# mLSTM gate maxima through DRAM and a broadcast DMA per head instead of TensorE products

## The chip, the cores and the metric

The kernel runs on one core of one Trainium2 chip. The metric is the device time of one execution in microseconds; for the kernel before it is the median of three runs. A core has five engines with a queue of instructions each: TensorE (PE, whose weight loads are shown as PEld), VectorE (DVE), ScalarE (ACT), GpSimd (POOL) and SyncE (SP). An engine takes its queue in order: an instruction that waits holds everything behind it. DMAs are issued from SP's queue (weights) and from POOL's (side loads, adding loads, reloads).

## The reference

One layer of a hybrid decoder on x of 512 tokens by 1024 columns, in fp32: a half-step SwiGLU, a mixer that runs dilated attention and an mLSTM side by side, and a second half-step SwiGLU. The change lies in the mLSTM, four heads of 256 columns:

```python
def step(carry, inp):                      # one chunk, all heads
    b = jnp.cumsum(ft, axis=-1)            # ft = log_sigmoid(forget gate), it = input gate
    D = jnp.where(causal, b[..., :, None] - b[..., None, :] + it[..., None, :], -jnp.inf)
    m_inter = b + m[..., None]
    m_t = jnp.maximum(m_inter, jnp.max(D, axis=-1))
    w = jnp.exp(D - m_t[..., None]) * jnp.einsum('bhtk,bhsk->bhts', qt, kt)
    inter = jnp.exp(m_inter - m_t)
    num = jnp.einsum('bhts,bhsv->bhtv', w, vt) + inter[..., None] * jnp.einsum('bhvk,bhtk->bhtv', C, qt)
    den = jnp.sum(w, axis=-1) + inter * jnp.einsum('bhk,bhtk->bht', n, qt)
    h = num / jnp.maximum(jnp.abs(den), jnp.exp(-m_t))[..., None]
```

The kernel treats the 512 tokens as one chunk. With F the running sum of the log forget gates and c = i - F, the weight of source s for target t is exp(c_s - G_t), where G_t is the running maximum of c (from 0); so all the weights of a head need G of every target on all 128 partitions that hold sources.

## The kernel before

The program is one long stream of TensorE work. Products are made in split precision: a matrix x is held as a rounded high part (xh, from a ScalarE cast) and a low part (xl, from a VectorE subtraction), and a product is xh·wh + xl·wh + xh·wl. Weights arrive by SP in slots wf (three), are cast into wh and wl (five of each), and are used 24 products at a time with 512 columns each. Two steps of a Strassen-like scheme save products in places, among them the value/gate projection of the mLSTM (`wide_seven`, tiles vo0p and vo1p, L940), which handles two heads at a time and adds blocks by accumulating DMAs on POOL's queue (vo_x0h, vo_x0l, vo_x; L894, L921).

What stands around the change, in order of the program:

- `gates()` (L1261) transposes the gate columns onto four partitions (one per head), computes F (Fc) and c (cc), and scans the running maxima Gm (L1275). Its tiles ga, gb4 and gc4 hold four partitions; gc4, which contains Gm, is the first tile of the tag gain, which has two buffers in the work pool. The second is selr: a selector matrix, loaded from in_sel, and beside it Gh, the rounded high part of Gm (L1276). Gl is the low part (L1277). The third tile of the tag is hg, the mLSTM gain (L1304), and the fourth and fifth are part5h and part5l (L1568), token parts that are reloaded from DRAM for the branch gates.
- `m_decay(h)` (L1404) spreads the head's row of maxima over 128 partitions with two products: selr has four rows, so selr's columns of head h times Gh, plus the same times Gl, gives G in all partitions of a PSUM bank pb. VectorE adds the causal mask (caus) into gd (L1409), one 128 x 128 square per diagonal block; ScalarE takes seven exponentials into E, four from gd (L1413) and three from pb (L1416), of 384, 256 and 128 columns, with c as bias.
- `m_scores(h)` (L1420) computes query-key products into three banks (pa), VectorE multiplies them into E, ScalarE casts Eh (L1435), VectorE subtracts El (L1436).
- `m_out(h)` (L1439) multiplies by the values (po), and VectorE, ScalarE and a small power on POOL (r_m, L1463) normalise; the squares go to a junk tile jm, which shares the one buffer of the tag gd. The result replaces so, and `m_turn(h)` transposes it on PE into pml (L1481).
- `m_qk_proj` and `m_qk_conv` (L1098, L1107) project (pm) and convolve the next head's queries and keys: z on ScalarE, three multiply-adds on VectorE, tanh, then the casts.

E has one buffer, in turn with the tile vo_E of the projection, so head 0's and head 2's exponentials can begin only when vo_E has been read. PSUM has eight banks in one ring of tiles: a new tile waits for the tile that was taken eight before it.

The kernel is written head by head (L1515 to L1573), but every engine's own order is set when the program is built: a scheduler lines up what is ready, subject to a few explicit orders (`issue_after`). Moving one operation can therefore move others.

Of the kernel before, what the change touches and what calls it, by code (L numbers as in the profile page):

```python
# [10 lines left out]
F32 = mybir.dt.float32  # L11
F32R = mybir.dt.float32r
BF16 = mybir.dt.bfloat16
AF = mybir.ActivationFunctionType
ALU = mybir.AluOpType

P = 128
T = 512
NT = T // P
D = 1024  # L20
# [8 lines left out]
MH = 4  # L29
# [10 lines left out]
def tile_hybrid_block(ctx: ExitStack, tc: tile.TileContext, a: dict):  # L40
    nc = tc.nc
# [16 lines left out]
    work = Work()  # L58
# [3 lines left out]
    def bank(name):  # L62
        return psum.tile([P, 512], F32, tag="pp", name=name)

    def pair(name):
        return [bank(f"{name}_{b}") for b in range(2)]
# [67 lines left out]
    dram = ctx.enter_context(tc.tile_pool(name="dram", bufs=1, space=bass.MemoryType.DRAM))  # L134
# [658 lines left out]
    mix = mctx.enter_context(tc.tile_pool(name="mix", bufs=1, side="right"))  # L793
# [15 lines left out]
    masks = ap_.tile([P, 512], BF16, name="masks")  # L809
    with tc.issue_after(mixer_from):  # L810
        nc.gpsimd.dma_start(masks, a["masks"])
    perm = ap_.tile([P, 2 * P + 8], F32, name="perm")
# [185 lines left out]
    def scores(h):  # L998
        q = [qk_of[h, g] for g in range(3)]
        ps0, ps1 = pair(f"ps0{h}"), pair(f"ps1{h}")  # L1000
        for tb in range(NT):
            lo = 0 if tb else P
            nc.tensor.matmul(ps0[tb // 2][:, tb % 2 * 256 + lo:(tb % 2 + 1) * 256], lhsT=q[0][:, 0, tb * P:(tb + 1) * P],
                             rhs=q[0][:, 1, max(tb - 1, 0) * P:(tb + 1) * P], start=True, stop=True)
        for g in (1, 2):
            for j in range(NT):
                o = j % 2 * 256 + (g - 1) * P
                nc.tensor.matmul(ps1[j // 2][:, o:o + P], lhsT=q[g][:, 0, j * P:(j + 1) * P], rhs=q[g][:, 1, j * P:(j + 1) * P], start=True, stop=True)
        sm = ap_.tile([P, 8, 256], F32, tag="sm", bufs=1, name=f"sm{h}")
        val = small.tile([P, 2, 8], F32, tag="val", name=f"val{h}")  # L1010
        nm = small.tile([P, 8], F32, tag="nm", name=f"nm{h}")
        for half, ps in enumerate((ps0, ps1)):
            for i in range(NT):
                lo = P if half == 0 and i == 0 else 0
                nc.vector.tensor_tensor_reduce(out=sm[:, 4 * half + i, lo:], in0=ps[i // 2][:, i % 2 * 256 + lo:(i % 2 + 1) * 256],
                                               in1=masks[:, half * 256 + lo:(half + 1) * 256], scale=1.0, scalar=NEG,
                                               op0=ALU.add, op1=ALU.max,
                                               accum_out=val[:, 0, 4 * half + i:4 * half + i + 1])
            hs = slice(4 * half, 4 * half + 4)
            nc.vector.tensor_scalar(nm[:, hs], val[:, 0, hs], -SC, None, op0=ALU.mult)  # L1020
        for i in range(8):
            lo = P if i == 0 else 0
            nc.scalar.activation(sm[:, i, lo:], sm[:, i, lo:], AF.Exp, scale=SC, bias=nm[:, i:i + 1],
                                 accum_out=val[:, 1, i:i + 1])
        return sm, val
# [227 lines left out]
    gi, lf = ga[:, 0, :], ga[:, 1, :]  # L1253
    Fc, cc = gb4[:, 0, :], gb4[:, 1, :]
    ones4, Gm = gc4[:, 0, :], gc4[:, 1, :]
    selr = work.tile([4, D], F32R, tag="gain", bufs=2, name="selr")
    Gh = selr[:, 512:1024]
    Gl = mix.tile([4, T], F32R, name="Gl")
    cT = mix.tile([P, 32], F32, name="cT")

    def gates():  # L1261
        pg = pair("pgate")
        for j in range(NT):
            for b in range(2):
                nc.tensor.transpose(pg[b][0:4, j * P:(j + 1) * P], gts[:, j, 4 * b:4 * b + 4], ident)
        nc.scalar.activation(gi, pg[0][0:4, :], AF.Identity, bias=gb[:, 0:1])
        nc.scalar.activation(Gm, pg[1][0:4, :], AF.Identity, bias=gb[:, 1:2])
        nc.vector.scalar_tensor_tensor(lf, Gm, -1.0, Gm, op0=ALU.mult, op1=ALU.max)
        nc.scalar.activation(lf, lf, AF.Exp, scale=-1.0)
        nc.scalar.activation(lf, lf, AF.Ln, bias=1.0)  # L1270
        nc.vector.scalar_tensor_tensor(lf, Gm, 0.0, lf, op0=ALU.min, op1=ALU.subtract)
        nc.vector.memset(ones4, 1.0)
        nc.vector.tensor_tensor_scan(Fc, ones4, lf, 0.0, op0=ALU.mult, op1=ALU.add)
        nc.vector.tensor_tensor(cc, gi, Fc, op=ALU.subtract)
        nc.vector.tensor_tensor_scan(Gm, cc, cc, 0.0, op0=ALU.max, op1=ALU.max)  # L1275
        nc.vector.tensor_copy(Gh, Gm)  # L1276
        nc.vector.tensor_tensor(Gl, Gm, Gh.bitcast(F32), op=ALU.subtract)  # L1277
        nc.vector.tensor_tensor(Fc, Fc, Gm, op=ALU.add)
        nc.scalar.activation(Fc, Fc, AF.Exp, scale=-1.0)

    def gates_turn():
        ptg = bank("ptg")
# [2 lines left out]
            nc.tensor.transpose(ptg[:, 16 + sb * 4:20 + sb * 4], Fc[:, sb * P:(sb + 1) * P], ident[0:4, 0:4])  # L1285
        nc.vector.tensor_copy(cT, ptg[:, 0:32])

    nc.gpsimd.dma_start(selr[:, 0:512], a["sel"])
    caus = mix.tile([P, 1, P], F32, name="caus")
    with tc.issue_after(mixer_from):  # L1290
        nc.gpsimd.dma_start(caus[:, 0, :], a["caus"])
    for h in range(1, HEADS):
        qk_proj(h, 0)
        exchange(h - 1, sm, val)
        qk_proj(h, 1)
        pT = turn(h - 1, sm)
        if h == 3:
            gates_turn()
        qk_proj(h, 2)
        values(h - 1, pT, v12s[(h - 1) // 2])  # L1300
        if h == 2:
            gates()
            hg = work.tile([P, 1, D], F32, tag="gain", bufs=2, name="hg")
            nc.gpsimd.dma_start(hg[:, 0, :], a["mlstm_head_g"].partition_broadcast(P))  # L1304
        sm, val = scores(h)
    pqs = [m_qk_proj(0, 0, lambda: exchange(3, sm, val))]
    tail = []
# [89 lines left out]
    def raw_o(h):  # L1397
        sos[h] = new_so(h)
        for j in range(NT):
            take_o(h, sos[h], j, raw[h][j // 2][:, j % 2, :])  # L1400

    OFF = (0, 512, 1024, 896)

    def m_decay(h):  # L1404
        gbc = bank(f"pb{h}")
        nc.tensor.matmul(gbc, lhsT=selr[:, h * P:(h + 1) * P], rhs=Gh, start=True, stop=False)
        nc.tensor.matmul(gbc, lhsT=selr[:, h * P:(h + 1) * P], rhs=Gl, start=False, stop=True)
        gd = mm.tile([P, NT, P], F32, tag="gd", bufs=1, name=f"gd{h}")
        nc.vector.tensor_tensor(gd, gbc.rearrange("p (a b) -> p a b", b=P), caus.broadcast_to([P, NT, P]), op=ALU.add)  # L1409
        E = mm.tile([P, 1280], F32, tag="E", bufs=1, name=f"E{h}")  # L1410
        for sb in range(NT):
            bias = cT[:, sb * 4 + h:sb * 4 + h + 1]
            nc.scalar.activation(E[:, OFF[sb]:OFF[sb] + P], gd[:, sb, :], AF.Exp, scale=-1.0, bias=bias)  # L1413
            n = T - (sb + 1) * P
            if n:
                nc.scalar.activation(E[:, OFF[sb] + P:OFF[sb] + P + n], gbc[:, (sb + 1) * P:], AF.Exp,  # L1416
                                     scale=-1.0, bias=bias)
        return E

    def m_scores(h, qk, E):  # L1420
        pa = [bank(f"pa{h}{i}") for i in range(3)]
        for sb in range(NT):
            n = T - sb * P
            out = pa[OFF[sb] // 512][:, OFF[sb] % 512:OFF[sb] % 512 + n]
            terms = [(x, y, dk) for x, y in ((0, 0), (0, 1), (1, 0)) for dk in range(2)]
# [255 lines left out]
def _consts():  # L1681
    half = 16
    inv = np.power(np.float32(500000.0), -(np.arange(half, dtype=np.float32) * np.float32(2.0) / np.float32(32.0)))
    ang = np.arange(T, dtype=np.float32)[None, :] * inv.astype(np.float32)[:, None]
    c, s = np.cos(ang).astype(np.float32), np.sin(ang).astype(np.float32)
    import ml_dtypes

    def rope(u, v):
        r = np.concatenate([u, v])
        return np.concatenate([r, r.reshape(32, P, 4).transpose(0, 2, 1).reshape(32, T)])[:, None, :]  # L1690

    p = np.arange(P)[:, None]
    i = np.arange(P)[None, :]
    masks = np.zeros((P, 512), np.float32)
    masks[:, 0:128] = np.where(p - (i - P) <= 128, 0.0, NEG)
    masks[:, 128:256] = np.where(p - i >= 0, 0.0, NEG)
    masks[:, 256:384] = masks[:, 128:256]
    masks[:, 384:512] = np.where((p - i >= 0) & ((p - i) % 4 == 0), 0.0, NEG)
    perm = np.zeros((P, 2 * P + 8), np.float32)
    c4 = np.arange(4)[None, :]  # L1700
    perm[:, 0:P] = p % 32 == i // 4
    perm[:, P:2 * P] = p // 4 == i % 32
    perm[:, 2 * P:2 * P + 4] = p % 4 == c4
    perm[:, 2 * P + 4:] = p // 32 == c4
    sel = np.zeros((4, MH * P), np.float32)
    for h in range(MH):
        sel[h, h * P:(h + 1) * P] = 1.0
    caus = np.where(np.arange(P)[None, :] >= p, 0.0, -NEG).astype(np.float32)
    return {
        "ropeC": rope(c, c), "ropeS": rope(-s, s),  # L1710
        "masks": masks.astype(ml_dtypes.bfloat16), "sel": sel, "caus": caus, "perm": perm,
    }


# [70 lines left out]
```

## Time and profile before

| | |
|---|---|
| median of the runs | 1314.66 us (1314.62 to 1315.81, 3 runs) |
| the profiled execution's own time | 1315.28 us |
| its span, first to last instruction | 1313.3 us |
| PE busy | 1305.4 us |
| VectorE busy | 1041.0 us |
| ScalarE busy | 657.9 us |
| GpSimd busy | 116.3 us |
| granted TensorE clock | 0.999 |
| data moved by DMA | 181.59 MB |

The span is what the trace shows; some 2 us of the execution lie around it. Rows of the timeline give the start in us, the duration, the engine, the line, the operation, the tiles (out<-in), the shape and how many were merged; in brackets stands how long the engine was idle before and what released it. Matmuls overlap, so the time that a matmul takes from the stream is the distance from its start to the next one's, not its duration. Lists of one tile give minimum, median and maximum of the durations in ns. Lists of DMA issues give the size and the median time from issue to landing.

### The profile page before, as it was taken

Reading aid. Unit: us, or ns where it says so; the run is one execution under the profiler, and the core shown is the slowest. Engines: PE = TensorE matmul, PEld = TensorE weight load, DVE = VectorE, ACT = ScalarE, POOL = GpSimd, SP = SyncE. Lnnn points to the kernel's source line nnn. Section 1 sums busy time; section 2 is a strip of 40 time slices with the busy share of each in tenths; the row PEclk is TensorE's granted clock in tenths of the full one; section 3 lists DMA queues with packets and bytes.
Section 4 is the critical chain, followed back from the end, with each engine's and each line's share of the span. In section 5 each row is a group of like instructions: output and inputs, shape, how many; then the busy total and the mean of one; then the engine's idle time right before and its main releaser. Section 6 shows DMA issues by size and latency. Waiting matters only on the chain.

```text
span 1313.3 us, 20816 instructions
## 1 busy us (share of the span) xinstructions
PE 1305.4 (99%) x8189; PEld 1180.7 (90%) x8189; DVE 1041.0 (79%) x1601; ACT 657.9 (50%) x1065; POOL 116.3 (9%) x168
## 2 busy tenths in 40 slices
PE   9999999999999999999999999999999999999997
PEld 9999999888898888888888889999889999999886
DVE  7999988788895575776797786776389999897887
ACT  6444454566644544635565464434265444445663
POOL 1000000231302100011002010000010000001220
PEclk9999999999999999999999999999999999999999
DMA  5333333796458922257627432235412333335981
GB/s 193 97 113 97 113 104 107 183 242 160 150 161 216 334 92 81 93 148 185 200 81 177 160 111 67 97 105 168 161 60 86 113 97 113 109 101 149 269 175 64
DMA packets 51473, 181.59 MB, mean 138 GB/s; under 512 B 5764, under 2 KB 6796, under 8 KB 51120
## 3 DMA queue, kind: packets, MB, share of 16 engines
q1 hardware_dynamic: 32832, 116.18, 26.2%
q0 software_dynamic: 18528, 64.09, 20.3%
q8 instruction: 64, 1.05, 0.3%
q14 instruction: 33, 0.27, 0.1%
q10 hardware_dynamic: 16, 0.00, 0.0%
HBM read 170.81 MB, written 9.44 MB: 137 GB/s over the span
## 4 chain that ended last, share of the span: by engine, by line
PE 99%; DVE 1%; POOL 0%; issue 0%; ACT 0%; DVEq 0%; POOLq 0%; ACTq 0%
PE qb_b L340 10%; PE qb_a L340 10%; PE pq L191 8%; PE pm L191 7%; PE qa_a L340 4%; PE qa_b L340 4%; PE qb_gm L1207 4%; PE acc_o L245 3%; PE accb_b L539 3%; PE vo1p L940 3%; PE vo0p L940 3%; PE w12p L940 3%; PE accb_a L539 3%; PE accc_b L539 2%; PE accc_a L539 2%; PE pg_a L205 2%
## 5 line engine op out<-in xcount | busy, mean ns | idle before, releaser
L191 PE MATMUL pq<-hTh_mx,wh_qk 128*128 128x512 f32 x160 | 63.2, 395 | 0.0
L191 PE MATMUL pq<-hTl_mx,wh_qk 128*128 128x512 f32 x160 | 62.4, 390 | 0.0
L101 DVE TENSOR_TENSOR wl_qk<-wf_qk,wh_qk 128x1024 fp32r<-128x1024 f32 x24 | 29.3, 1222 | 26.6 <-PE pq L191 18.9
L191 PE MATMUL pm<-hTh_mx,wh_mqk 128*128 128x512 f32 x128 | 50.4, 394 | 0.0
L191 PE MATMUL pm<-hTl_mx,wh_mqk 128*128 128x512 f32 x128 | 49.9, 390 | 0.0
L85 ACT CAST wh_qk<-wf_qk 128x1024 fp32r<-128x1024 f32 x24 | 25.0, 1047 | 33.5 <-PE pq L191 12.1
L265 ACT CAST wh_a<-cd_a 128x1024 fp32r<-128x1024 f32 x19 | 19.9, 1049 | 40.8 <-DVE cd_a L265 40.8
L265 ACT CAST wh_b<-cd_b 128x1024 fp32r<-128x1024 f32 x19 | 19.9, 1049 | 40.6 <-DVE cd_b L265 40.6
L191 PE MATMUL pq<-hTh_mx,wl_qk 128*128 128x512 f32 x160 | 39.5, 389 | 0.0
L340 PE MATMUL qa_a<-hTh_f,wh_a 128*128 128x256 f32 x152 | 38.2, 284 | 0.0
L340 PE MATMUL qa_b<-hTh_f,wh_b 128*128 128x256 f32 x152 | 38.2, 284 | 0.0
L340 PE MATMUL qa_a<-hTl_f,wh_a 128*128 128x256 f32 x152 | 38.1, 283 | 0.0
L340 PE MATMUL qa_b<-hTl_f,wh_b 128*128 128x256 f32 x152 | 38.1, 283 | 0.0
L1115 DVE SCALAR_TENSOR_TENSOR z<-pm,cw,z 128x511 f32<-128x511 f32 (+2 forms) x48 | 35.3, 744 | 2.2 <-ACT z L1113 1.8
L191 PEld LDWEIGHTS pq<-hTh_mx,wl_qk 128*128 128x128 f32 x160 | 30.0, 188 | 6.2
L191 PEld LDWEIGHTS pq<-hTh_mx,wh_qk 128*128 128x128 f32 x160 | 30.1, 188 | 6.0
L191 PEld LDWEIGHTS pq<-hTl_mx,wh_qk 128*128 128x128 f32 x160 | 30.1, 188 | 6.0
L265 DVE TENSOR_TENSOR wl_b<-ab_b,wh_b 128x1024 fp32r<-128x1024 f32 x19 | 23.3, 1225 | 15.0 <-ACT wh_b L265 15.0
L265 DVE TENSOR_TENSOR wl_a<-ab_a,wh_a 128x1024 fp32r<-128x1024 f32 x19 | 23.3, 1225 | 14.7 <-ACT wh_a L265 14.7
L265 POOL DMA_DIRECT2D T_a<-in_wdq x12 | 11.1, 1184 | 239.4 <-DVE xl_a L265 229.0
L265 POOL DMA_DIRECT2D T_b<-in_wdq x12 | 10.8, 1156 | 235.3 <-PE acca_b L539 225.7
L191 PE MATMUL pm<-hTh_mx,wl_mqk 128*128 128x512 f32 x128 | 31.6, 389 | 0.0
(1025 smaller groups left out, 4644.1 us busy)
## 6 DMA issues: line engine op xcount, KB each, us to landing
wf_qk<-in_wqk SPq DMA_DIRECT2D x24, 512.0 KB, 3.3
g_a<-in_wgu SPq DMA_DIRECT2D x19, 512.0 KB, 3.7
u_a<-in_wgu SPq DMA_DIRECT2D x19, 512.0 KB, 3.7
g_b<-in_wgu SPq DMA_DIRECT2D x19, 512.0 KB, 3.7
u_b<-in_wgu SPq DMA_DIRECT2D x19, 512.0 KB, 3.7
wf_mqk<-in_wmqk SPq DMA_DIRECT2D x16, 512.0 KB, 3.7
wf_vo<-in_wvo SPq DMA_DIRECT2D x16, 512.0 KB, 3.9
T_a<-in_wdq POOLq DMA_DIRECT2D x12, 512.0 KB, 10.7
```

Source lines behind the costliest of these rows:

```text
L85: return nc.scalar.copy(wh, wf)
L101: last_low[0] = nc.vector.tensor_tensor(wl[:, :m], wf[:, :m], wh[:, :m].bitcast(F32), op=ALU.subtract).ins
L191: nc.tensor.matmul(out, lhsT=wt[:, k * P:(k + 1) * P], rhs=x[:, k, 0:T], start=n == 0, stop=n == len(terms) - 1)
L205: nc.tensor.matmul(outs[b][:, tok], lhsT=ws_[b][w][:, k * P:(k + 1) * P], rhs=x[:, k, tok], start=i + k + hf == 0, stop=hf == 1 and i == 2 ...
L245: nc.tensor.matmul(out, lhsT=x[:, tk], rhs=w[:, cs], start=first and n == 0, stop=last and n == 2, skip_group_check=True)
L265: self.last[eng] = getattr(getattr(nc, eng), fn)(*args, **kw).ins
L340: nc.tensor.matmul(out, lhsT=wt[:, i * P:(i + 1) * P], rhs=y[:, i, :], start=first and n == 0, stop=last and n == len(terms) - 1, skip_gro ...
L539: nc.tensor.matmul(o, lhsT=x[:, tk], rhs=w[:, cs], start=k in "1256" and g + m + n == 0, stop=False, skip_group_check=True)
L940: nc.tensor.matmul(out[k][i], lhsT=x[:, 2 * g + m, i * P:(i + 1) * P], rhs=y[:, m * T:(m + 1) * T], start=k in "156" and g + m + j == 0, s ...
L1115: nc.vector.scalar_tensor_tensor(z[:, s:], src[:, :T - s], cw[:, ct, 3 - s:4 - s], z[:, s:], op0=ALU.mult, op1=ALU.add)
L1207: nc.tensor.matmul(out, lhsT=wt[:, i * P:(i + 1) * P], rhs=y[:, i, :], start=first and m == 0, stop=last and m == len(terms) - 1, skip_gro ...
```

## The change

The two products per head, selr, Gh, Gl and the bank pb are gone. Instead `gates()` writes Gm to a DRAM tile gmax, and `load_gmax(h)` reads a head's row back into all 128 partitions of an SBUF tile gbc, 512 fp32 values each. gbc has one buffer; head 0's is loaded directly behind `gates()`, each later one is issued where the previous head's `m_decay` ends. All of these DMAs are issued from POOL's queue. The mask addition and the three exponentials read gbc.

```diff
-    selr = work.tile([4, D], F32R, tag="gain", bufs=2, name="selr")
-    Gh = selr[:, 512:1024]
-    Gl = mix.tile([4, T], F32R, name="Gl")
+    gmax = dram.tile([4, T], F32, name="gmax")
...
         nc.vector.tensor_tensor_scan(Gm, cc, cc, 0.0, op0=ALU.max, op1=ALU.max)
-        nc.vector.tensor_copy(Gh, Gm)
-        nc.vector.tensor_tensor(Gl, Gm, Gh.bitcast(F32), op=ALU.subtract)
+        nc.gpsimd.dma_start(gmax, Gm)
         nc.vector.tensor_tensor(Fc, Fc, Gm, op=ALU.add)
...
+    def load_gmax(h):
+        g = mix.tile([P, T], F32, tag="gbc", bufs=1, name=f"gbc{h}")
+        nc.gpsimd.dma_start(g, gmax[h].partition_broadcast(P))
+        return g
...
-    nc.gpsimd.dma_start(selr[:, 0:512], a["sel"])
...
             nc.gpsimd.dma_start(hg[:, 0, :], a["mlstm_head_g"].partition_broadcast(P))
+            gbc = load_gmax(0)
...
+    gmaxes = {0: gbc}
...
     def m_decay(h):
-        gbc = bank(f"pb{h}")
-        nc.tensor.matmul(gbc, lhsT=selr[:, h * P:(h + 1) * P], rhs=Gh, start=True, stop=False)
-        nc.tensor.matmul(gbc, lhsT=selr[:, h * P:(h + 1) * P], rhs=Gl, start=False, stop=True)
+        gbc = gmaxes.pop(h)
...
+        if h + 1 < MH:
+            gmaxes[h + 1] = load_gmax(h + 1)
         return E
```

The scheduler's order changes with it. On TensorE, at head 1's place, between the second half of the projection of head 1's keys (pm) and the transposes of head 0's result (pml), before:

```order
L191 MATMUL pm_1_6740<-hTl_mx,wh_mqk_6749 128x512
L191 MATMUL pm_1_6740<-hTh_mx,wl_mqk_6751 128x512 x8
L1406 MATMUL pb_6815<-selr 128x512
L1407 MATMUL pb_6815<-Gl,selr 128x512
L1481 MATMUL pml_0_6840<-ident,so_6424 128x128
L1481 MATMUL pml_1_6841<-ident,so_6424 128x128
```

Now the transposes follow the projection directly, and the other heads' pairs are gone in the same way; nothing else of TensorE's order is changed. On GpSimd's queue, from the gain's load to the first loads of the value/gate projection:

```order
 L989 DMA v12rows_4917<-v12flat_4640 128x2x512
 L993 DMA v_1_4920<-v12rows_4917 128x2048
-L1304 DMA hg<-in_mlstm_head_g 128x1024
+L1305 DMA hg<-in_mlstm_head_g 128x1024
+L1274 DMA gmax<-gc_4967 4x512
+L1280 DMA gbc_5616<-gmax 128x512
+L1172 DMA part5h<-kept5h 128x1024
 L894 DMA vo_x0h<-in_wvo 128x1024
 L894 DMA vo_x0l<-in_wvo 128x1024
```

The write, head 0's broadcast and part5h have come in here; part5h stood before behind head 2's powers, and takes gc4's buffer now, since hg has that of selr. Of the later broadcasts head 1's stands ahead of the loads vo_x of the second pair, head 2's behind head 0's two powers, and head 3's behind the two loads of part4m, ahead of head 2's powers. On ScalarE, from head 0's exponentials (E_6506, gbc_5616 is head 0's, gbc_6514 head 1's) to head 1's convolution, now:

```order
L1417 ACTIVATE E_6506<-gbc_5616,cT 128x128
L1414 ACTIVATE E_6506<-gd_6504,cT 128x128
L85 CAST wh_mqk_6747<-wf_mqk_6745 128x1024
L85 CAST wh_mqk_6866<-wf_mqk_6864 128x1024
L1438 CAST Eh_6569<-E_6506 128x512 x2
L1438 CAST Eh_6569<-E_6506 128x256
L1417 ACTIVATE E_6815<-gbc_6514,cT 128x384
L1417 ACTIVATE E_6815<-gbc_6514,cT 128x256
L1417 ACTIVATE E_6815<-gbc_6514,cT 128x128
L85 CAST wh_mqk_6872<-wf_mqk_6870 128x1024
L1113 ACTIVATE z_6646<-pm_0_6584,cw 128x512
```

Head 1's three exponentials that read gbc have moved ahead of a weight cast; before, all seven of head 1 stood some 25 rows later, with the transposes of head 0. The four that read gd now come after head 0's squares, and the same happens with head 3's behind head 2's Eh. On VectorE the mask addition of heads 1 and 3 stands directly behind the variance (vv) of the normalisation of heads 0 and 2, ahead of the scale rr and of the low part vml, which before came first.

More of the change, by code (lines that the diff above doesn't have):

```diff
@@ L1704, in _consts @@
     perm[:, 2 * P + 4:] = p // 32 == c4
-    sel = np.zeros((4, MH * P), np.float32)
-    for h in range(MH):
-        sel[h, h * P:(h + 1) * P] = 1.0
     caus = np.where(np.arange(P)[None, :] >= p, 0.0, -NEG).astype(np.float32)
@@ L1710, in _consts @@
         "ropeC": rope(c, c), "ropeS": rope(-s, s),
-        "masks": masks.astype(ml_dtypes.bfloat16), "sel": sel, "caus": caus, "perm": perm,
+        "masks": masks.astype(ml_dtypes.bfloat16), "caus": caus, "perm": perm,
     }
```

## The prediction

> **What bounds the kernel now.** I read the page first (busy shares, chain), then busy times by stretch, then PE's timeline around the four products to be removed.
>
> ```profile
> span 1313.3 us, 20816 instructions
> ...
> PE 1305.4 (99%) x8189; PEld 1180.7 (90%) x8189; DVE 1041.0 (79%) x1601; ACT 657.9 (50%) x1065; POOL 116.3 (9%) x168
> ...
> PE 99%; DVE 1%; POOL 0%; issue 0%; ACT 0%; DVEq 0%; POOLq 0%; ACTq 0%
> ```
>
> The chain that ended last is PE for 99%. The mLSTM part, where the change lies, has no hole at all: in the row below (window and length, then PE, PEld, DVE, ACT and POOL busy) PE is busy 300.00 of 300 us, VectorE 228.97, ScalarE 160.07.
>
> ```profile
> 530.00:830.00 300.00, 300.00 (x1578) 256.58 (x1577) 228.97 (x419) 160.07 (x291) 29.88 (x41) 1.00 0.48 135
> ```
>
> So a microsecond taken out of PE's stream there comes off the end, unless another engine then makes PE wait. Nothing else that the change takes away can shorten anything directly.
>
> **The change part by part.**
>
> *The eight products.* A busy PE in the trace is overlapped matmuls, so the cost of one is read from start to start. Head 0's, then head 1's, then a place where the same kinds of neighbours meet with nothing between them:
>
> ```profile
> 633.28 0.62 PE L940 MATMUL vo0p<-wh_vo,hTl_mx 128*128 128x512 f32 x2
> 633.73 0.61 PE L940 MATMUL vo0p<-wl_vo,hTh_mx 128*128 128x512 f32 x2
> 634.28 0.49 PE L1406 MATMUL pb<-selr 4*128 4x512 f32 x1
> 634.61 0.39 PE L1407 MATMUL pb<-Gl,selr 4*128 4x512 f32 x1
> 634.94 1.19 PE L940 MATMUL vo0p<-wh_vo,part 128*128 128x512 f32 x4
> ...
> 636.43 1.07 PE L940 MATMUL vo0p<-wh_vo,part 128*128 128x512 f32 x4
> ```
>
> ```profile
> 668.80 1.07 PE L191 MATMUL pm<-hTh_mx,wl_mqk 128*128 128x512 f32 x4
> 669.80 0.49 PE L1406 MATMUL pb<-selr 4*128 4x512 f32 x1
> ...
> 670.46 1.09 PE L1481 MATMUL pml<-ident,so 128*128 128x128 f32 x8
> 671.30 0.47 PE L191 MATMUL pm<-hTh_mx,wh_mqk 128*128 128x512 f32 x1
> ```
>
> ```profile
> 713.77 0.62 PE L940 MATMUL vo1p<-wl_vo,hTh_mx 128*128 128x512 f32 x2
> 714.23 1.03 PE L1481 MATMUL pml<-ident,so 128*128 128x128 f32 x8
> 715.02 1.17 PE L940 MATMUL vo1p<-wh_vo,part 128*128 128x512 f32 x4
> ```
>
> Two ordinary 512-column products take 633.73 - 633.28 = 0.45 us, 0.227 each. Head 0: without its pair the next product would start at 633.73 + 0.45 = 634.18; it starts at 634.94, which is 0.76, and its first group of four lasts 1.19 instead of the usual 1.07, another 0.12. Together 0.88 us. Head 1: four products from 668.80 end their slots at 668.80 + 0.91 = 669.71; the transposes start at 670.46, which is 0.75, and take 671.30 - 670.46 = 0.84 to the next product, where the place without a pair takes 715.02 - 714.23 = 0.79. Together 0.80. That the direct passage is free is seen there: 714.23 - 713.77 = 0.46, two plain slots. Heads 2 and 3 stand in the same surroundings:
>
> ```profile
> L1406 PE MATMUL pb<-selr x4: 494/494/494, 634.3 to 769.8; 4*128 4x512 f32 x4
> L1407 PE MATMUL pb<-Gl,selr x4: 392/392/392, 634.6 to 770.1; 4*128 4x512 f32 x4
> ```
>
> ```profile
> 733.72 0.61 PE L940 MATMUL vo1p<-wl_vo,hTh_mx 128*128 128x512 f32 x2
> ...
> 734.92 0.97 PE L940 MATMUL vo1p<-wh_vo,part4m 128*128 128x512 f32 x3
> ```
>
> ```profile
> 768.33 1.52 PE L191 MATMUL pm<-hTh_mx,wl_mqk 128*128 128x512 f32 x6
> ...
> 770.44 1.09 PE L1481 MATMUL pml<-ident,so 128*128 128x128 f32 x8
> ```
>
> Head 2: 734.92 - 733.72 - 0.45 = 0.75, with the same 0.12 it is 0.87. Head 3: 770.44 - 768.33 - 6 x 0.227 = 0.75, with head 1's 0.05 it is 0.80. Sum 0.88 + 0.80 + 0.87 + 0.80 = **3.3 us**. Bounds: only the eight plain slots, 8 x 0.227 = 1.8 us; all time in which the two lines are shown busy, 4 x (0.494 + 0.392) = 3.5 us. I take 3.3, since it comes from the same neighbours with and without the pair.
>
> *One PSUM bank fewer per head.* The banks go round in turn, so every later tile takes a bank that was given up earlier: it can only shorten waits, and PE shows none here. Nothing.
>
> *Exponentials and the causal add read SBUF.* Both kinds of reading stand in the trace, minimum, median and maximum in ns:
>
> ```profile
> L1416 ACT ACTIVATE E<-pb,cT x12: 343/462/567, 638.8 to 773.5; 128x384 f32<-128x384 f32 x4, 128x256 f32<-128x256 f32 x4, 128x128 f32<-128x128 f32 x4
> L1413 ACT ACTIVATE E<-gd,cT x16: 391/396/403, 638.5 to 773.7; 128x128 f32<-128x128 f32 x16
> ```
>
> At 128 columns PSUM takes 343 ns and SBUF 396, so the twelve become about 53 ns longer each, 0.6 us on ScalarE, which is busy 160 of 300 us: covered. If that cover were gone, it would cost at most those 0.6 us. The Trainium skill ("Perfetto Trace Analysis", section "Optimizing Scalar/DVE Operations") speaks against the change here: it gives ScalarE an access overhead of some 93 ns on SBUF and 51 on PSUM. The trace's 53 ns is near that difference of 42; by the page the twelve would cost an estimated 0.5 us, also off the path. The causal add and the two removed VectorE operations on four partitions are likewise VectorE work beside a full PE.
>
> *The write and the first broadcast on GpSimd's queue, and part5h.* They stand between the gain load and the first load of the value/gate projection, whose issue is released much later:
>
> ```profile
> 539.95 0.55 POOL L1304 DMA_DIRECT2D hg<-in_mlstm_head_g  x1 [84.64 <-DVE Gl L1277]
> 574.03 0.53 POOL L894 DMA_DIRECT2D vo_x0h<-in_wvo  x1 [33.52 <-DVE nm L1020]
> ```
>
> ```profile
> hg<-in_mlstm_head_g POOLq DMA_DIRECT2D x1, 512.0 KB, 4.2
> part7ml<-kept7l POOLq DMA_DIRECT2D x1, 512.0 KB, 12.4
> ```
>
> The maxima are ready before 539.95, since Gl was computed from them by then. The write is tiny and the broadcast moves 256 KB, half of the gain; a transfer of this queue landed within 4.2 us (quiet) to 12.4 us (crowded). Write and read in turn, with 0.55 of issue each, are done after 2 x 4.75 = 9.5 us, at about 549; even with 12.4 it is 566. The queue is free again before 574.03. The early part5h needs only the gates' buffer and is merely loaded long before its use. Cost nothing; cover at least 8 us.
>
> *The three later broadcasts.* Each waits for the last reader of the one tile gbc, so the GpSimd queue stops there. Behind gbc1 stand the next pair's loads vo_x, behind gbc2 a chain of the same pair, behind gbc3 head 2's small powers, which themselves need head 2's exponentials and so can't be held. In the trace of before:
>
> ```profile
> 640.49 0.40 ACT L1413 ACTIVATE E<-gd,cT 128x128 f32<-128x128 f32 x1
> ...
> 646.14 0.62 ACT L1435 CAST Eh<-E 128x512 fp32r<-128x512 f32 x1 [1.37 <-DVE E L1433]
> 648.15 1.05 ACT L85 CAST wh_mqk<-wf_mqk 128x1024 fp32r<-128x1024 f32 x1 [1.39 <-PE pm L191]
> ```
>
> ```profile
> 640.98 1.11 POOL L894 DMA_DIRECT2D vo_x<-in_wvo  x2 [26.27 <-PE vo0p L940]
> ```
>
> ```profile
> 681.16 1.04 ACT L256 CAST wh_vo<-vo_x 128x1024 fp32r<-128x1024 f32 x1
> ```
>
> Head 0's last exponential ends at 640.89 and vo_x was issued at 640.98: it slips by one issue, some 0.6 us, and is first cast at 681.16. Covered. For gbc1 the new ScalarE order matters: three of head 1's exponentials now stand directly behind head 0's last Eh cast, which ends at 646.76, about 645.9 once PE is 0.9 earlier. gbc1 is there at 640.89 + 0.55 + 4.2 = 645.6 in the quiet case, just in time, and at 653.8 in the crowded one. ScalarE then stands, and behind it the next weight cast (was 648.15). PE needs that weight only here:
>
> ```profile
> 664.27 0.39 PE L191 MATMUL pm<-hTh_mx,wh_mqk 128*128 128x512 f32 x1
> ```
>
> that is 663.4 after the shift. From 653.8, the three exponentials (under 1.5 us) and the cast (1.05) end at 656.4: 7 us before it. Head 3 repeats this behind gbc3. I put it at nothing, with 0 to 0.5 us for a ScalarE that comes late elsewhere.
>
> *The causal add of heads 1 and 3 ahead of the normalisation.* On VectorE it now stands where vml stood, before the scale that PE's transposes wait for:
>
> ```profile
> 665.22 0.42 DVE L1350 TENSOR_TENSOR vml<-vo_m1l,vmh 128x256 fp32r<-128x256 f32 x1
> 666.23 0.16 DVE L1467 TENSOR_TENSOR rr<-r_m,dn 128x2 f32<-128x2 f32 x1 [0.59 <-POOL r_m L116]
> 666.42 0.88 DVE L1470 SCALAR_TENSOR_TENSOR so<-po,rr,so 128x256 f32<-128x256 f32 x2
> ```
>
> rr waits 0.59 us for GpSimd anyway, which takes the longer add; vml moved behind rr delays the end of so from 667.30 to 667.7. The transposes would now start at 669.71 by head 1's arithmetic (PE and this chain both shift by head 0's 0.9): 2.0 us of room are left. This is the tightest place. Nothing.
>
> **Sum.** The profiled execution took 1315.28 us, so it would become 1312.0. The median of the runs, 1314.66, lies 0.6 below it: 1314.66 - 3.3 = **1311.4**.
>
> **The rivals.**
>
> *A. The slow passage stays in part or one head's gain is lost (same).* The passage around the pair costs 0.1 us at either edge, and a late result from VectorE may take a head's share. Left are the 1.8 us of plain slots: 1312.8, 0.14% less. For it: PE is so full that every other engine runs only just ahead of it. Against: the direct passage at 713.77 shows plain slots. The Trainium skill ("TensorE: Matmul & The Clock Gate", section "Back-to-back issue gap") has N/2.4 + 2.5 ns for an isolated product on a warm array: an estimated 216 ns at 512 columns, eight of them 1.7 us, the time of this rival. The trace disagrees: the pair's starts lie 0.33 us apart (634.28, 634.61, 634.94) where plain ones take 0.227.
>
> *B. A broadcast comes too late and stops PE through ScalarE (slower).* The place is gbc1 and gbc3, the queue ScalarE's. It decides when the landing takes longer than 663.4 - 2.5 - 641.4 = 19.5 us; each microsecond beyond that is PE's, twice. At 24 us it would be 2 x 4.5 - 3.3 = 5.7 us slower: 1320. For it: ScalarE's order was moved so that one wait holds everything; 11 to 12 us are on record. Against: the crowded landings had four large loads ahead in the queue, gbc1 has none. The Trainium skill ("SBUF — State Buffer", section "SBUF: two separate sides") says that VectorE's two-port modes keep GpSimd from writing descriptors, which would lengthen just these DMAs; no row here separates that from queueing.
>
> **How the numbers follow.** Under 0.2%, 2.6 us, a measurement of this kernel can't tell a difference from no change. Forecast 0.69: 3.3 us with its own 2.8 to 3.5, that is 1311.2 to 1311.9, all faster. A 0.22: same. B 0.09: slower. The range takes in the most that the pairs can give with the scatter of the runs (1314.66 - 3.5 - 0.7 = 1310.5) and A with as much above (1312.8 + 0.7 = 1313.5); B is left out.
>
> **What would show it.** PE's starts run on at 0.227 us where the pairs stood; vo0p to part and pm to pml pass directly; PE busy is about 3 us less; the mLSTM stretch is still full. ScalarE waits for gbc at most a few microseconds, in head 1 and 3. I am wrong if PE shows holes after 640 or 740 that end in a ScalarE or VectorE release, or if the passages cost the same without the pairs.

## The result and the profile after

| | before | after |
|---|---|---|
| median of 13 runs each | 1315.43 us (1314.58 to 1319.06) | 1312.38 us (1311.21 to 1314.09) |
| the profiled execution | 1315.28 us | 1311.85 us |
| its span | 1313.3 us | 1309.8 us |

The ratio is 0.9975 with a 95% interval of 0.9967 to 0.9983: the kernel is faster by 0.25%, some 3.3 us (2.2 to 4.3). The forecast was 1311.4 us from a median of 1314.66; the 13 runs of before, which include the three behind that median, have a median 0.8 us higher. The two medians lie 3.05 us apart where 3.3 were forecast.

First the page of after, and its busy times in the stretch of the mLSTM (window and length, then PE, PEld, VectorE, ScalarE and GpSimd busy):

```profile
span 1309.8 us, 20797 instructions
...
PE 1301.5 (99%) x8181; PEld 1178.9 (90%) x8181; DVE 1038.2 (79%) x1599; ACT 658.4 (50%) x1065; POOL 119.1 (9%) x172
```

```profile
530.00:830.00 300.00, 300.00 (x1599) 259.18 (x1598) 227.77 (x417) 161.39 (x292) 32.85 (x45) 1.00 0.49 139
```

TensorE has eight instructions less and is still busy 300.00 of 300 us. What it gained shows between two fixed marks of its stream, the first product of vo0p and the first of p_0a:

```profile
601.27 0.70 PE L940 MATMUL vo0p<-wh_vo,hTh_mx 128*128 128x512 f32 x2
...
633.57 0.62 PE L940 MATMUL vo0p<-wl_vo,hTh_mx 128*128 128x512 f32 x2
634.02 1.07 PE L940 MATMUL vo0p<-wh_vo,part 128*128 128x512 f32 x4
...
666.84 1.98 PE L191 MATMUL pm<-hTh_mx,wl_mqk 128*128 128x512 f32 x8
668.66 1.04 PE L1484 MATMUL pml<-ident,so 128*128 128x128 f32 x8
...
782.48 0.45 PE L191 MATMUL p_0a<-atth,wh_wA 128*128 128x512 f32 x1
```

The same marks in before:

```profile
601.44 0.70 PE L940 MATMUL vo0p<-wh_vo,hTh_mx 128*128 128x512 f32 x2
...
786.05 0.45 PE L191 MATMUL p_0a<-atth,wh_wA 128*128 128x512 f32 x1
```

The stretch takes 782.48 - 601.27 = 181.21 us instead of 786.05 - 601.44 = 184.61: 3.40 us less, nearly all of the span's 3.5. From vo0p to part it is now 634.02 - 633.57 = 0.45, two plain slots, and the group of four lasts 1.07 and no longer 1.19. Eight products of pm lead directly to the transposes: 668.66 - 666.84 = 1.82, eight slots of 0.227. By head the shift of TensorE's starts is 0.88, 0.81, 0.88 and 0.81 us.

The broadcast now, with its readers (duration minimum, median and maximum in ns) and its landing:

```profile
L1417 ACT ACTIVATE E<-gbc,cT x12: 384/494/617, 636.7 to 745.8; 128x384 f32<-128x384 f32 x4, 128x256 f32<-128x256 f32 x4, 128x128 f32<-128x128 f32 x4
...
DMA to landing us min/median/max: 3.4/4.4/4.9
```

GpSimd's queue and ScalarE's around head 1's broadcast:

```profile
538.09 0.51 POOL L1274 DMA_DIRECT2D gmax<-gc  x1 [82.62 <-DVE two L1035]
540.10 0.57 POOL L1280 DMA_DIRECT2D gbc<-gmax  x1 [1.50 <-DMA gmax<-gc]
540.66 0.55 POOL L1172 DMA_DIRECT2D part5h<-kept5h  x1
573.88 0.53 POOL L894 DMA_DIRECT2D vo_x0h<-in_wvo  x1 [32.67 <-DVE nm L1020]
...
639.79 0.57 POOL L1280 DMA_DIRECT2D gbc<-gmax  x1 [25.26 <-ACT E L1414]
```

```profile
644.88 0.93 ACT L1438 CAST Eh<-E 128x512 fp32r<-128x512 f32 x2 [1.72 <-DVE E L1436]
646.60 1.31 ACT L1417 ACTIVATE E<-gbc,cT 128x384 f32<-128x384 f32 x3 [0.79 <-DVE El L1439]
```

Issued at 639.79, a broadcast that takes 4.9 at most is there by 644.7. ScalarE comes to it at 645.81 (644.88 + 0.93) and waits 0.79 us for VectorE's El, not for the DMA. So nothing waits for a broadcast in heads 1 and 3, and the queue of GpSimd is idle for 32.67 us ahead of vo_x0h.

### The profile page after: what moved, and what is told of

The parts are those of the page before. It is cut to its first block, busy times and chain, and to the rows that moved or that the text cites. A ratio compares the mean times of both kernels' runs of the same rounds, so it can differ in the third digit from the quotient of the medians.

```text
span 1309.8 us, 20797 instructions
## 1 busy us (share of the span) xinstructions
PE 1301.5 (99%) x8181; PEld 1178.9 (90%) x8181; DVE 1038.2 (79%) x1599; ACT 658.4 (50%) x1065; POOL 119.1 (9%) x172
## 4 chain that ended last, share of the span: by engine, by line
PE 98%; DVE 1%; DMA 0%; POOL 0%; ACT 0%; issue 0%; DVEq 0%; POOLq 0%; ACTq 0%
PE qb_a L340 10%; PE qb_b L340 10%; PE pq L191 8%; PE pm L191 7%; PE qa_b L340 4%; PE qa_a L340 4%; PE qb_gm L1207 4%; PE acc_o L245 3%; PE accb_b L539 3%; PE w12p L940 3%; PE vo1p L940 3%; PE vo0p L940 3%; PE accb_a L539 3%; PE accc_b L539 2%; PE accc_a L539 2%; PE pg_a L205 2%
## 5 line engine op out<-in xcount | busy, mean ns | idle before, releaser
L85 ACT CAST wh_qk<-wf_qk 128x1024 fp32r<-128x1024 f32 x24 | 25.0, 1046 | 32.8 <-PE pq L191 12.1
```

Of the source, the lines that this page charges most:

```text
L85: return nc.scalar.copy(wh, wf)
```

## The experiments

The theory is that the whole gain is TensorE's time, 0.86 us per pair, and that everything else stays covered. Two questions were put to the chip: what the products cost and of what that consists, and how late a broadcast may come until the gain is lost, and through which wait. "The stretch" is the one between the two marks above, read from one profiled execution of each kernel; ratios are to runs of before on the same chip as the experiment.

### What the products cost

**pairs_back** puts two products of four rows per head back into after, into a bank that nothing reads; the rest of the change stays.

```diff
         gbc = gmaxes.pop(h)
+        pb = bank(f"pb{h}")
+        for i in range(N):                      # N = 2, R = 4
+            nc.tensor.matmul(pb, lhsT=hTh[0:R, 4, 0:P], rhs=hTh[0:R, 5, 0:T], start=i == 0, stop=i == N - 1)
```

> The changed kernel with two four-row products of 512 columns per head put back at the old places, into a bank that nobody reads; the maxima still come by the broadcast, and nothing of the result is changed. Theory (PE's slots are the whole gain): the 3.3 us come back, 1315.4 or 1.000 of the kernel before, and the starts at the pairs lie 0.33 us apart as before. Rival (the gain came from what moved with the change: a bank less, the early part5h, ScalarE's new order): most of the gain stays, 1312.4 to 1313.5 us. Rival A of the prediction (only plain slots count): 1312.4 + 1.8 = 1314.2.

It took 1315.5 us, a ratio to before of 0.9998 (0.9990 to 1.0007), and the stretch 787.75 - 603.21 = 184.54 us, which is before's 184.61. The two products, with the bank that they take, bring back all that the change gained; that the bank alone costs nothing shows in ten_full below, whose 40 products cost their plain slots and no more. What else the change did (the DMAs, the exponentials that read SBUF, the new orders) is worth nothing that this can tell, which is 0.1% either way.

**one_product** is before without the low part: Gl, its subtraction and the second product are left out, so the maxima have only their rounded high part.

```diff
-        nc.tensor.matmul(gbc, lhsT=selr[:, h * P:(h + 1) * P], rhs=Gh, start=True, stop=False)
-        nc.tensor.matmul(gbc, lhsT=selr[:, h * P:(h + 1) * P], rhs=Gl, start=False, stop=True)
+        nc.tensor.matmul(gbc, lhsT=selr[:, h * P:(h + 1) * P], rhs=Gh, start=True, stop=True)
```

> The kernel before without the second product of each pair; the low part of the gate maxima is left out, so they are rounded. PE's slots: by the starts of before (0.33 for the second product) it saves 4 x 0.33 = 1.3 us, 1314.1; if only plain slots counted, 4 x 0.227 = 0.9 us, 1314.5; the trace tells the two apart by the starts. If the gain of the change were not PE's, nothing: 1315.4.

1314.65 us, a ratio of 0.9988 (0.9979 to 0.9996). The stretch is 786.98 - 603.28 = 183.70 us, 0.91 less than before: 4 x 0.227. The interval of the ratio is too wide to tell this from the 1.3 us of four starts of 0.33; the stretch is not. So the second product of a pair costs a plain slot, and what remains of the pair beside two slots, some 0.40 us, is paid once, by the passage.

**ten_small**, **ten_full** and **ten_half** are pairs_back with N = 10 and R = 4, 128 and 64 rows.

> The same with ten four-row products per head instead of two, into an unread bank. If each such product costs 0.33 us from start to start, the block takes 3.3 us a head and the time is 1312.4 + 13.5 = 1325.9. If only the passages into and out of the block are slow (about 0.1 us each and one slow first start) and the products inside run at 0.227, the block takes 2.6 us a head: 1312.4 + 10.3 = 1322.7.

> The same ten products per head with all 128 rows instead of four. If the slow starts belong to four-row operands, these run at 0.227 without slow passages: 9.1 us in all, 1321.5. If they belong to any foreign product put between two groups, the time is that of the ten four-row products.

> Ten products per head with 64 of 128 rows, into an unread bank. With four rows the block had four slow starts (0.09 to 0.11 us each: into it, after its first, out of it, after the next) and the granted clock fell to 0.66 behind two of the four blocks; with 128 rows neither. If any partial use of the rows brings the slow starts, this block takes 2.67 us a head, 1312.4 + 10.7 = 1323.1, and with a lower clock up to 3.3 us more; if 64 rows are enough for plain slots, 1312.4 + 9.1 = 1321.5.

| kernel | time | ratio to before | stretch | above after | 40 x 0.227 + passages |
|---|---|---|---|---|---|
| ten_full | 1322.09 us | 1.0048 (1.0035 to 1.0062) | 190.27 us | 9.06 | 9.08 + 0 |
| ten_half | 1323.22 us | 1.0063 (1.0047 to 1.0078) | 191.97 us | 10.76 | 9.08 + 4 x 0.40 |
| ten_small | 1327.49 us | 1.0080 (1.0067 to 1.0092) | 195.23 us | 14.02 | 9.08 + 4 x 0.40 + 3.3 |

The rows of head 0 in the three, in this order ten_full, ten_half, ten_small; the distance between the starts of the block and of the product behind it is the block's time:

```profile
633.89 0.62 PE L940 MATMUL vo0p<-wl_vo,hTh_mx 128*128 128x512 f32 x2
634.34 2.43 PE L1411 MATMUL pb<-hTh_mx 128*128 128x512 f32 x10
636.61 1.07 PE L940 MATMUL vo0p<-wh_vo,part 128*128 128x512 f32 x4
```

```profile
634.12 0.61 PE L940 MATMUL vo0p<-wl_vo,hTh_mx 128*128 128x512 f32 x2
634.67 2.58 PE L1411 MATMUL pb<-hTh_mx 64*128 64x512 f32 x10
637.18 1.20 PE L940 MATMUL vo0p<-wh_vo,part 128*128 128x512 f32 x4
```

```profile
633.53 0.61 PE L940 MATMUL vo0p<-wl_vo,hTh_mx 128*128 128x512 f32 x2
634.08 2.66 PE L1411 MATMUL pb<-hTh_mx 4*128 4x512 f32 x10
636.67 2.08 PE L940 MATMUL vo0p<-wh_vo,part 128*128 128x512 f32 x4
```

With all 128 rows the block takes 636.61 - 634.34 = 2.27 us, ten slots of 0.227, and the way in is 0.45 for two: no passage at all. With 64 rows it takes 2.51, the way in 0.55, and the group behind it lasts 1.20 instead of 1.07. So the surcharge belongs to the change between products of fewer rows (4 and 64 here) and full ones, and not to a foreign weight or bank. Inside the block the starts of four rows lie some 0.23 us apart, as those of 128 do: my expectation of 0.33 us for every product was wrong, 0.33 is what both products of a pair show because both stand at an edge. The Trainium skill ("TensorE: Matmul & The Clock Gate", section "Why this matters for your kernels") says that one product of 32 rows takes the same time as one of 128. For 4 and 64 rows the trace agrees inside a block; at the edges it is 0.40 us more per block.

ten_small's remaining 3.3 us are the clock. The third column from the right is the granted clock, ten_small first, then ten_half, in the same window at the end of head 0's block:

```profile
636.45:639.86 3.41, 3.41 (x9) 2.52 (x9) 1.28 (x2) 2.38 (x7) 0.11 (x1) 0.50 0.31 100
```

```profile
636.45:639.86 3.41, 3.41 (x16) 2.54 (x15) 1.87 (x4) 2.77 (x9) 0.00 (x0) 1.00 0.19 48
```

TensorE is busy throughout in both, yet ten_small has 9 products in it where ten_half has 16, since the granted clock was 0.50 for these 3.41 us (a mean of 0.66 over 636 to 641, the figure in the expectation of ten_half). It fell so at heads 0 and 2 and not at 1 and 3: twice 3.41 us at half the clock lose 3.4 us. Ten products of four rows in a row, 2.6 us, were enough for it there, two were not.

### How late a broadcast may come

The next kernels leave everything of after as it is, each engine's order too, and only make the broadcast slow: the maxima are laid out in DRAM so that each partition's 2048 bytes are read in pieces.

```diff
-    gmax = dram.tile([4, T], F32, name="gmax")
+    gmax = dram.tile([T // C, 4, C], F32, name="gmax")     # C = 64, 16, 8: pieces of 256, 64, 32 bytes
...
-        nc.gpsimd.dma_start(gmax, Gm)
+        nc.gpsimd.dma_start(gmax.rearrange("k h c -> h k c"), Gm.rearrange("p (k c) -> p k c", c=C))
...
-        nc.gpsimd.dma_start(g, gmax[h].partition_broadcast(P))
+        nc.gpsimd.dma_start(g.rearrange("p (k c) -> p k c", c=C), gmax[:, h, :].partition_broadcast(P))
```

In pieces_16 (C = 4) and pieces_8 (C = 2) a broadcast is two and four such DMAs, of 256 and 128 columns.

> The changed kernel with the maxima laid out in DRAM so that each partition's 2 KB arrive in 8 pieces of 256 bytes; the instructions and their order on all engines are the same, only the write and the four broadcasts are slower. Theory (the broadcasts are covered until head 1's lands some 19.5 us after its issue): the landing gets longer than 4.4 us, the time stays at 1312.4. Rival (the broadcasts are only just in time, every microsecond of landing is PE's): the time grows by the extra landing, at least once.

> The same with 32 pieces of 64 bytes, four times as many. Theory: as long as the landing stays under 19.5 us the time stays at 1312.4 us; if it is longer, ScalarE stands on head 1's and head 3's broadcast and PE loses the excess twice. Rival (just in time): the excess over 4.4 us is lost in full in heads 1 and 3, so 10 us of landing would give 1323.

> The same with 64 pieces of 32 bytes. Theory: landing about twice that of the 64-byte pieces; past 19.5 us the excess is lost in heads 1 and 3 (a landing of 30 us: 1312.4 + 2 x 10.5 = 1333), with the holes in PE's stream behind a ScalarE that waits for the broadcast; below it nothing. Rival (just in time): twice the excess over 4.4 us, 1363 at 30 us.

> The changed kernel with the maxima in 16-byte pieces, each broadcast as two DMAs of 64 pieces a partition, since 64 pieces of 32 bytes landed after 11.8 us without any loss. From there the landing should double, to some 22 us, and GpSimd takes about 5.6 us to issue the two. Theory (PE stops when head 1's broadcast lands later than 19.5 us after its issue): the first holes, 2.5 us in each of heads 1 and 3, 1312.4 + 5 = 1317. Rival (a point earlier than that decides, or GpSimd's blocked queue, behind which vo_x and the small powers stand): more, 1320 or over, with holes that end on another release. Third possibility: no loss yet, 1312.4, if ScalarE makes up for it.

> The same in 8-byte pieces, four DMAs of 64 pieces a partition for each broadcast: landing some 42 us after the first issue. Theory: ScalarE stands on head 1's and head 3's broadcast for some 38 us, PE loses what goes beyond 19.5 us, 2 x 22 us, about 1357 us, the holes ending on ScalarE's weight cast. Rival (the broadcasts can't stop PE at all): 1312.4.

| kernel | median landing of one DMA | ScalarE's wait for gbc, heads 1 and 3 together | time | ratio to before |
|---|---|---|---|---|
| after | 4.4 us | none | 1312.38 us | 0.9975 (0.9967 to 0.9983) |
| pieces_256 | 5.0 us | none | 1311.69 us | 0.9970 (0.9959 to 0.9982) |
| pieces_64 | 6.8 us | 1.7 us, all in head 1 | 1312.49 us | 0.9974 (0.9965 to 0.9984) |
| pieces_32 | 11.8 us | 11.4 us | 1312.03 us | 0.9973 (0.9963 to 0.9983) |
| pieces_16 | 10.0 us, two in turn | 31.1 us | 1335.46 us | 1.0152 (1.0135 to 1.0169) |
| pieces_8 | 14.6 us, four in turn | 106.0 us | 1465.2 us | 1.113 (1.1105 to 1.1155) |

Up to 12 us from issue to landing nothing is lost, though ScalarE stands for 5.7 us in each of two heads. pieces_16 was expected to lose some 5 us by the prediction's point of 19.5 us; its stretch is 806.08 - 601.71 = 204.37, a loss of 23.2. Its waits (total, times, longest), then TensorE, VectorE and a row of GpSimd:

```profile
ACT E L1421 <- DMA gbc<-gmax: 31.1, 2, 15.6
...
PE pml L1488 <- DVE so L1477: 17.6, 4, 6.4
```

```profile
667.28 1.98 PE L191 MATMUL pm<-hTh_mx,wl_mqk 128*128 128x512 f32 x8
675.62 1.09 PE L1488 MATMUL pml<-ident,so 128*128 128x128 f32 x4 [6.37 <-DVE so L1477]
679.20 1.11 PE L1488 MATMUL pml<-ident,so 128*128 128x128 f32 x4 [2.49 <-DVE so L1477]
...
680.54 0.63 PE L191 MATMUL pm<-hTl_mx,wh_mqk 128*128 128x512 f32 x1
680.97 0.63 PE L191 MATMUL pm<-hTh_mx,wh_mqk 128*128 128x512 f32 x1
```

```profile
664.15 1.23 DVE L101 TENSOR_TENSOR wl_mqk<-wf_mqk,wh_mqk 128x1024 fp32r<-128x1024 f32 x1 [17.15 <-ACT wh_mqk L85]
...
678.26 0.16 DVE L1474 TENSOR_TENSOR rr<-r_m,dn 128x2 f32<-128x2 f32 x1 [0.59 <-POOL r_m L116]
...
678.67 0.87 DVE L1477 SCALAR_TENSOR_TENSOR so<-po,rr,so 128x256 f32<-128x256 f32 x2
```

```profile
673.95 0.82 POOL L116 TENSOR_TENSOR r_m<-vv,nhalf 128x2 f32<-128x2 f32 x1 [7.01 <-DVE vv L1469]
```

TensorE never waits for the weight: it stands at the transposes of the previous head's result. VectorE is the carrier. It stood 17.15 us for the weight cast behind the broadcast on ScalarE, and everything queued behind that subtraction came late with it: the convolution, the denominators, the squares, rr and so. The rival on record, GpSimd's blocked queue, is not it: that queue stood ready for 7.01 us until VectorE gave it vv. Behind the holes the products start 0.43 us apart (680.97 - 680.54) for about eight products, at a granted clock of 0.50. The new theory: from the start of the exponentials to the second so is a fixed chain, and the second four transposes are due at a fixed time. In pieces_16 the exponentials began at 661.87 and the second transposes at 679.20, 17.33 us later. In pieces_32 the broadcast's issue, the exponentials and the transposes were:

```profile
640.85 2.80 POOL L1281 DMA_DIRECT2D gbc<-gmax  x1 [24.84 <-ACT E L1415]
```

```profile
652.97 1.31 ACT L1418 ACTIVATE E<-gbc,cT 128x384 f32<-128x384 f32 x3 [5.68 <-DMA gbc<-gmax]
```

```profile
670.14 1.04 PE L1485 MATMUL pml<-ident,so 128*128 128x128 f32 x8
```

652.97 + 17.33 = 670.30, and the second four were due at 670.14 + 0.40 = 670.54: pieces_32 had 0.24 us to spare. Its broadcast was issued at 640.85, so 12.12 us lay from issue to the exponentials, and the point lies at about 12.4.

pieces_8 was expected at about 1357 us and took 1465.2. The chain is there again (the exponentials of head 1 at 726.72, the second transposes at 744.04, 17.32 later), but it is no test of this wait alone: TensorE waited 92.4 us at the transposes, 24.3 for ScalarE's copy vo_m1h, which stands behind casts of the late load vo_x, and 15.7 for the load part5mh. Both loads are issued behind four broadcasts in GpSimd's queue, so here that queue is a carrier too.

Two kernels were made to fall between 12.4 and 19.5, with columns 0 to 255 in pieces of 16 bytes and columns 256 to 511 in pieces of 64 or 32:

```diff
-        nc.gpsimd.dma_start(g, gmax[h].partition_broadcast(P))
+        for i, c in enumerate(C):                # C = (4, 16) or (4, 8), H = T // 2
+            nc.gpsimd.dma_start(g[:, i * H:(i + 1) * H].rearrange("p (k c) -> p k c", c=c),
+                                gmax[i][:, h, :].partition_broadcast(P))
```

> The broadcast of each head is split into two: columns 0 to 255 in pieces of 16 bytes, columns 256 to 511 in pieces of 64 bytes. No result is changed and no engine's order but for the additional DMAs on GpSimd's queue. In pieces_16 two of the slow halves landed 9 to 12 us behind one another; here the second half should take some 5 us, so the landing is estimated at 14 to 18 us from the first issue, between 12.0 (pieces_32, no loss) and 22.1 (pieces_16, 23.2 us lost). What was on record before the run (weight cast, point at 19.5 us): nothing lost, 1312.4. New theory (the second so of the normalisation is 17.4 us behind the landing, 661.77 to 679.20 in pieces_16, and in pieces_32 652.89 + 17.4 = 670.3 just ahead of the second four transposes at 670.5, so the point lies at about 12.4 us): each microsecond of landing above 12.4 is PE's, in head 1 and in head 3, idle time that ends on so; for 16 us of landing 2 x 3.6 = 7.2 us in the stretch, about 1319.6, and up to 2 us more per head where the hole is long enough for the granted clock to drop behind it.

> As mixed_16_64, with the second half in pieces of 32 bytes: some 1.5 us later, estimated at 15 to 19.5 us. On record before: nothing lost, 1312.4. New theory: 2 x (landing - 12.4), for 17.5 us 10.2 us, about 1322.6, and up to 2 us more per head for the clock. The difference to mixed_16_64 should be twice the difference of the two landings.

They took 1316.82 us, a ratio of 1.0002 (0.9992 to 1.0013), and 1318.2 us, 1.0017 (1.0005 to 1.0029): the gain of 0.25% is gone in the first, and more than that in the second. The mixed kernels also have one more DMA for the write and one for each broadcast in GpSimd's queue. ScalarE and TensorE in mixed_16_64, whose broadcast of head 1 was issued at 641.51 and that of head 3 at 743.42:

```profile
655.81 1.31 ACT L1423 ACTIVATE E<-gbc,cT 128x384 f32<-128x384 f32 x3 [7.88 <-DMA gbc<-gmax]
...
757.27 1.31 ACT L1423 ACTIVATE E<-gbc,cT 128x384 f32<-128x384 f32 x3 [7.27 <-DMA gbc<-gmax]
```

```profile
670.78 0.60 PE L1490 MATMUL pml<-ident,so 128*128 128x128 f32 x4
673.15 1.04 PE L1490 MATMUL pml<-ident,so 128*128 128x128 f32 x4 [1.77 <-DVE so L1479]
...
772.85 0.60 PE L1490 MATMUL pml<-ident,so 128*128 128x128 f32 x4
774.61 0.83 PE L1490 MATMUL pml<-ident,so 128*128 128x128 f32 x4 [1.16 <-DVE so L1479]
```

From issue to exponentials it is 14.30 and 13.85 us, less than I had estimated. By the point of 12.4, 1.9 + 1.45 = 3.35 us should be lost; the second transposes come 2.37 - 0.40 = 1.97 and 1.76 - 0.40 = 1.36 late, 3.33 together, with the wait ending on so. The chain is 673.15 - 655.81 = 17.34 us. In mixed_16_32 the distances are 14.97 and 14.81, the sum 4.98, and the transposes came 2.14 and 2.30 us late, 4.44 together; the chain in head 1 is 17.34 again. The stretches, 186.54 and 187.86 us, are 5.33 and 6.65 above after; of the 2.0 and 2.2 us beyond the lateness 1.7 are the clock, which was granted at 0.50 for 3.41 us behind one of the two holes in each. The profiled execution of mixed_16_64 is the slowest of its ten (1319.06 us), so that share need not be in every one. The theory on record, the weight cast at 19.5 us, would have let both pass without loss: it has fallen. The new one was made from 12.1 and 22.2 us; at the four distances between, it gave 3.35 and 4.98 us for the two kernels, and 3.33 and 4.44 were measured.

## Why the prediction was right, point by point

**The pairs.** 3.3 us forecast, 3.40 in the stretch; by head 0.88, 0.80, 0.87 and 0.80 forecast, 0.88, 0.81, 0.88 and 0.81 measured. Taking start-to-start distances from the same neighbours with and without a pair was the step that carried it. Rival A's eight plain slots, 1.8 us, miss the passages: 4 x 0.40 = 1.6 us, which pairs_back, one_product and ten_full show between them. The isolated gap of the Trainium skill ("TensorE: Matmul & The Clock Gate", section "Back-to-back issue gap"), an estimated 216 ns, lies near one slot (0.227 here) and holds nothing of the passages.

**Exponentials from SBUF.** 384 ns instead of 343 at the least, 494 instead of 462 in the middle and 617 instead of 567 at the most: 32 to 50 ns each, forecast 53, and covered, since pairs_back is no slower than before. The difference of 42 ns that the Trainium skill gives ("Perfetto Trace Analysis", section "Optimizing Scalar/DVE Operations") lies among them.

**Write, first broadcast, part5h.** The write landed in 1.7 us where 4.2 were allowed for, and the queue then stood idle for 32.67 us ahead of vo_x0h. Covered as forecast.

**The later broadcasts.** They landed in a median of 4.4 us where the prediction took 4.2 from the nearest quiet landing, and head 1's was there by 644.7 where 645.6, "just in time", had been forecast. No wait for it.

**The causal add ahead of the normalisation.** The place with 2.0 us of room:

```profile
664.17 0.68 DVE L1410 TENSOR_TENSOR gd<-gbc,caus 128x512 f32<-128x512 f32 x1
665.44 0.16 DVE L1470 TENSOR_TENSOR rr<-r_m,dn 128x2 f32<-128x2 f32 x1 [0.59 <-POOL r_m L116]
665.85 0.87 DVE L1473 SCALAR_TENSOR_TENSOR so<-po,rr,so 128x256 f32<-128x256 f32 x2
```

so ends at 666.72, the transposes start at 668.66: 1.9 us, as forecast.

**What failed: Rival B's price and place.** The prediction let a late broadcast stop TensorE "through ScalarE" at the next weight, and put the point at 19.5 us of landing. The runs show it at about 12.4, at the transposes, through ScalarE and VectorE together. I had followed ScalarE's queue one step, to the cast, and had asked only TensorE when it needs that weight; VectorE needs the cast first, for the low part, and holds the normalisation behind it. The tightest place, which the paragraph on the causal add had found, was not connected with this wait. The 19.5 was misread even for TensorE: the product at 664.27 does not use that weight. In pieces_16 its counterpart runs while the cast that was held up is still going on:

```profile
663.09 1.03 ACT L85 CAST wh_mqk<-wf_mqk 128x1024 fp32r<-128x1024 f32 x1
```

```profile
663.65 0.39 PE L191 MATMUL pm<-hTh_mx,wh_mqk 128*128 128x512 f32 x1
```

Counted through the sixteen casts of wh_mqk, each used for 24 products, the held-up one is the tenth, and TensorE starts on the tenth group at 675.00 in after, 11.6 us later than the prediction's 663.4. The price was too low as well: at 22.2 us each head lost 9.7 us at the transposes where 2.7 would be beyond the old point, and the lower clock took nearly 2 more in each. It did not matter for the forecast only because the landing was 4.4 us. The room of the change is thus 12.4 less 4.9, some 7.5 us and not the 14.6 that 19.5 would leave, and a crowded landing like the 12.4 us of before's part7ml would have used all of it.

**What stays open.** Why the passage to and from products of fewer rows costs four starts of 0.10 us more is not shown, only that 4 and 64 rows do it and 128 don't. That the granted clock drops behind some holes of about 2 us and behind two of ten_small's four blocks, and not behind the others, was seen and not explained.

## What to carry to other kernels

On a full TensorE, price a small product by the distance between the starts around it, with and without it, never by its rows or its busy time: here 4 and 64 rows cost a full slot each, and each block of them an edge of 0.40 us on top. When an operation is moved behind a DMA on one engine, follow the wait through the queues of every engine that takes something from behind it, to the first place where TensorE needs any of it; the nearest consumer is not always the tightest. A cover is worth testing by making the covered thing slower until it shows: here it was half of what the reading of the queues had given.

## What was not expected of the hardware

**Pieces of a broadcast.** The same 256 KB landed in a median of 4.4, 5.0, 6.8 and 11.8 us in pieces of 2048, 256, 64 and 32 bytes, and its issue took GpSimd 0.57, 0.94, 1.74 and 2.81 us. In pieces_16 the second DMA of a pair was issued 9.70 us after the first's issue ended:

```profile
639.65 2.81 POOL L1283 DMA_DIRECT2D gbc<-gmax  x1 [24.68 <-ACT E L1418]
652.16 2.77 POOL L1283 DMA_DIRECT2D gbc<-gmax  x1 [9.70 <-issue]
```

With a smaller second half it followed at once (two issues in 3.99 us from 641.51 in mixed_16_64). The Trainium skill ("DMA: Bandwidth & Descriptors", section "Anatomy of one DMA — SWDGE (gpsimd) path") fits 2.0 us plus the bytes by 436 GB/s, an estimated 2.6 us for this size; the runs show 4.4 with whole rows.

**The clock.** TensorE's granted clock fell to 0.50 for 3.41 us at two of four blocks of ten products of four rows without any hole (ten_small), and behind holes of 1.77 (mixed_16_64) and 2.10 us (mixed_16_32), but not behind those of 1.16 and 1.94 in the same two kernels. The Trainium skill ("TensorE: Matmul & The Clock Gate", section "Why this matters for your kernels") warns of gaps above some 3 us; here shorter ones were enough.
